# Adaptive modulation units spread into the attention output projection, weight splits by transfer alone, and token blocks formed by ScalarE in a two-layer diffusion trunk on one core

## The chip, the core and the metric

One core of a Trainium2 chip runs the whole program. The metric is the device time of one execution in microseconds, as a median over runs. TensorE (PE) multiplies matrices; VectorE (DVE), ScalarE (ACT) and GpSimd (POOL) do elementwise work. SyncE (SP) and POOL here also issue transfers, each from a queue that it works off in order.

## The reference, cut to what matters

The trunk has two layers over 512 latent and 128 context tokens, 640 columns in all, with a width of 1024. Every sub-layer is modulated by nine vectors that come from the condition, and ends in a LayerNorm:

```python
mod = (silu(cond) @ ada_w[i] + ada_b[i]).reshape(-1, 9, 1024)
x = layer_norm(a*x + 0.5*mod[:, 2]*swiglu(modulate(x, mod[:, 0], mod[:, 1])), ...)
x = layer_norm(a*x + mod[:, 5]*mixer(modulate(x, mod[:, 3], mod[:, 4])), ...)   # attention, or Hyena
x = layer_norm(a*x + 0.5*mod[:, 8]*swiglu(modulate(x, mod[:, 6], mod[:, 7])), ...)
```

Each feed-forward multiplies by w1 (1024 to 2 x 2816), forms silu(g)*u, and multiplies by w2 (2816 to 1024). All arithmetic is in float32.

## The kernel before, in words

**Precision and weights.** Each float32 product is three matmuls: high part by high part, high by low, and low by high. A weight unit is one tile of the stream `units`, for w1 128 x 2048 (1 MB), and it needs a high tile `wh` and a low tile `wl` out of a ring of 8 buffers. The usual way (L120, L137, L138): POOL issues a load that casts to the high part (`wh`), ACT writes its negative into `wl`, and POOL issues a second transfer of the same weights that adds the original onto it. For the odd blocks 3 to 17 of the second feed-forward of layer 0 (`PLAIN`, 8 units) it is done otherwise: SP loads the unit plainly into a third buffer `wr`, ACT casts it to `wh` (L96), and DVE subtracts to get `wl` (L97), in two halves.

**Order.** The schedule is written out by hand; every engine runs its instructions in the order in which the program emits them. `w_get` keeps up to three units split ahead. Small chains (a LayerNorm) are woven into the matmul loops with `at(delay, key, fn)`, by a clock of modelled matmul time, and `flush(key)` emits what is still pending.

**Stages.** Filter spectra; feed-forward (0,0); attention with its output projection (`proj`); feed-forward (0,1); the first feed-forward of layer 1 (`ffn_s(0)`); Hyena with its projection; the last feed-forward (`ffn_s(1)`). A w1 unit is used twice, for token halves 0 and 1, and each use is a step of 48 matmuls. The first three units run half 0 first and half 1 after that (steps 0 to 5), so that the LayerNorm of half 1 has time.

**Modulation units.** One unit is a 128 x 1024 block of `ada_w` (512 KB, tile `ar`, two buffers) that POOL loads (L253) and DVE multiplies and sums against the condition with two instructions (L267), one for latents and one for context. `bg_step` does one unit and asks POOL for the next but one; that request can only go out when DVE has finished with the buffer, and whatever POOL has queued behind it waits too. Feed-forward (0,0) does 56 units (one after each step from block 3 on, and one after each pair of w2 groups); feed-forward (0,1) does 72, with two after each pair of w2 groups in its first two parts. The pool `fq` of that second batch (with `cond`, 1 MB, loaded anew and put through Silu by ACT, L261) is opened when `proj` is done.

**Layer 1's feed-forwards** run the first three w1 blocks in the ordinary way, then w2 for them (`second`, 16 groups of 9 matmuls), and all further blocks by a Strassen-like scheme with 7 products in place of 8. It needs four combinations of token blocks, which `s_tokens(k)` forms for k = 0 to 3: POOL adds high and low parts back to float32 (L596, 4 adds for each k), DVE makes 4 sums and differences (L598 to L601), and 4 splits follow (ACT L96, DVE L97). The calls come after steps 3, 4 and 5, and the last one inside `second`. The LayerNorm's own scale and bias (`s4`, L403, DVE) are put on x after 50 us of modelled time or at the flush ahead of `second`, whose residual updates (L515) need them.

Of the kernel before, what the change touches and what calls it, by code (L numbers as in the profile page):

```python
# [9 lines left out]
F32 = mybir.dt.float32  # L10
F32R = mybir.dt.float32r
# [4 lines left out]
P = 128  # L16
# [4 lines left out]
KD = 8  # L21
# [1 line left out]
NF = 22  # L23
PARTS = [(0, 6), (6, 12), (12, 18), (18, 22)]

PLAIN = range(3, 18, 2)
PARTS7 = [(0, 3), (3, 6), (6, 9), (9, 12), (12, 15), (15, 18), (18, 22)]
ALPHA = 4.0 ** 0.25
EPS = 1e-5
# [16 lines left out]
class Kernel:  # L46
# [63 lines left out]
    def w_dma(self, upto):  # L110
        nc = self.nc
        while self.wd < min(upto, self.wlim):
            i = self.wd
            src, shape, plain = self.units[i]
            if plain:
                r = self.wp.tile(shape, F32, tag="w", name="wr")
                nc.sync.dma_start(out=r, in_=src)
            else:
                r = self.wp.tile(shape, F32R, tag="w", name="wh")
                nc.gpsimd.dma_start(out=r, in_=src)  # L120
            self.raw[i] = r
            self.wd += 1

    def w_split(self):
        i = self.ws
        if i >= self.wlim:
            return
        self.w_dma(i + 1)
        shape, plain = self.units[i][1:]
        hi = self.raw.pop(i)  # L130
        lo = self.wp.tile(shape, F32R, tag="w", name="wl")
        if plain:
            raw, hi = hi, self.wp.tile(shape, F32R, tag="w", name="wh")
            for k in (slice(0, KD // 2), slice(KD // 2, KD)):
                self.split(hi[:, k], lo[:, k], raw[:, k])
        else:
            self.nc.scalar.activation(out=lo, in_=hi.bitcast(F32), func=AF.Copy, scale=-1.0)  # L137
            self.nc.gpsimd.dma_start(out=lo, in_=self.units[i][0], accum_op=ALU.add)  # L138
        self.wt[i] = (hi, lo)
        self.wlive.add(i)  # L140
        self.ws += 1
        self.w_dma(i + 3)

    def w_first(self):

        i = self.wd
        src, shape = self.units[i][:2]
        self.raw[i] = self.wp.tile(shape, F32, tag="w", name="wr")
        self.nc.sync.dma_start(out=self.raw[i], in_=src)
        self.wd += 1  # L150
# [199 lines left out]
    def ln_sched(self, l, i, half, sum_t, GB):  # L350
        nc = self.nc
        a, z = HALF[half]
        C = (z - a) // 4
        key = f"ln{half}"
        when = LNT[min(2 * l + i, 2)][half]
        st = {}

        def s1():
            mu = self.ps(name="mu")
            nc.tensor.matmul(mu[:, 0:320], self.ones_mean, sum_t)  # L360
            sq = {}
# [12 lines left out]

            self.interleave([[lambda k=k: centre(k), lambda k=k: square(k), lambda: None, lambda k=k: add(k)] for k in range(KD)])
            (nc.vector if half else nc.gpsimd).tensor_tensor(out=sq[4], in0=sq[0], in1=sq[4], op=ALU.add)
            st["q"] = sq[4]

        def s2():
            vp = self.ps(name="vp")  # L380
            for c in range(4):
                nc.tensor.matmul(vp[:C, c:c + 1], st["q"][:, c * C:(c + 1) * C], self.ones_mean[:, 0:1])
            st["dg"] = self.rstd(vp, C)

        def s3():
            r = self.ps(name="rs")
            for c in range(4):
                nc.tensor.matmul(r[:, c * C:(c + 1) * C], self.ones[:C, :], st["dg"][:, c, :])
            if half == 0:
                self.h = []  # L390
            G, B = GB

            def scale(k):
                xk = self.x[:, k, a:z]
                nc.vector.tensor_tensor(out=xk, in0=xk, in1=r[:, 0:320], op=ALU.mult)

            self.interleave([[lambda k=k: scale(k)] + self.h_stages(half, k, self.x[:, k, :], G, B) for k in range(KD)],
                            key, when[3])

        def s4():  # L400
            for k in range(KD):
                xk = self.x[:, k, a:z]
                nc.vector.tensor_scalar(out=xk, in0=xk, scalar1=self.lnga[:, l, i, k:k + 1],  # L403
                                        scalar2=self.lnba[:, l, i, k:k + 1], op0=ALU.mult, op1=ALU.add)

        for t, f in zip(when, (s1, s2, s3)):
            self.at(t, key, f)
        self.at(50, key + "x", s4)

    def ln_out(self, l, i, half, sum_t):  # L410

# [175 lines left out]
    def s_tokens(self, k):  # L587

        nc = self.nc
        B = {}  # L590
        for r in range(2):
            hh, hl = self.h[k + 4 * r]
            for c in range(2):
                cs = slice(320 * c, 320 * c + 320)
                B[r, c] = self.t((P, 320), name="sb")
                nc.gpsimd.tensor_tensor(out=B[r, c], in0=hh[:, cs].bitcast(F32), in1=hl[:, cs].bitcast(F32), op=ALU.add)  # L596
        t1, t3, t2, t4 = B[0, 0], B[0, 1], B[1, 1], B[1, 0]
        nc.vector.tensor_tensor(out=t1, in0=t3, in1=t1, op=ALU.subtract)  # L598
        nc.vector.tensor_tensor(out=t3, in0=t2, in1=t3, op=ALU.subtract)
        nc.vector.tensor_tensor(out=t2, in0=t2, in1=t1, op=ALU.subtract)  # L600
# [119 lines left out]
    def ffn_s(self, f, u0):  # L720
# [27 lines left out]
        acts = {}  # L748
        self.wlim = u + 5
        steps = self.group_steps(range(u, u + 3), lambda w, q, half, u=u: self.ffn1(acts, q - u, sact)(w, q, half))  # L750
        for n, s in enumerate(steps):
            self.run_steps([s])
            if n == 2:
                self.s_load(3, 0)
                self.s_load(3, 1)
            if n > 2:
                self.s_tokens(n - 3)
        self.flush("ln0x")
        self.flush("ln1x")
        gt = self.gate(l, 2 + 3 * (2 if f else 0), 0.5)  # L760
        w = self.s_weights(3, 4)
        second(u + 3, acts, gt, {1: lambda: self.s_tokens(3), 6: w[0], 8: w[1], 10: w[2], 12: w[3]})
        u += 5
        for pi, (c0, c1) in enumerate(PARTS7[1:]):
            fin = pi == 5
            acts = {}
            for i in range(3):
# [7 lines left out]
                    w = self.s_weights(c + 1, after[c + 1])  # L775
                    hooks = {0: w[0], 1: w[1], 3: w[2], 5: w[3]}
                if i == 1:
                    hooks[2] = lambda m=u + 1: cast(m)
                    hooks[3] = lambda m=u + 2, w=w: (w[2](), cast(m))
                if i == 2:  # L780
                    hooks[0] = self.w_split
# [37 lines left out]
    def ffn(self, l, f, u0):  # L819
# [8 lines left out]
        for pi, part in enumerate(PARTS):  # L828
# [2 lines left out]
            c = part[0]  # L831
            while c < part[1] - fin:
                n = 3 if c == 0 else 1
                self.run_steps(self.group_steps(range(u, u + n), lambda w, q, half, d=c - u: ffn1(q + d)(w, q, half)), c > 0)
                u += n
                c += n
            if pi == 0:
# [4 lines left out]
            if not fin:  # L842
                for jj in range(4):
                    w = self.w_get(u)
                    for j2 in range(2):
                        for half in range(2):
                            ps = self.ps(name="f")
                            self.mm_cols(ps, w, j2 * P, acts, ks, half)
                            self.resid(ps, jj * 2 + j2, half, gt)
                        self.bg_step()  # L850
                        if pi < 2 and f:
                            self.bg_step()
                    self.w_done(u)
                    u += 1
            else:
# [6 lines left out]
                def fn(w, q, half, u=u, c=c):  # L862
# [11 lines left out]
                        self.ln_out(l, i_ln, half, sums[half])  # L874
                    elif j == 7:
                        self.ln_sched(l, i_ln, half, sums[half], GB)
                self.run_steps(self.group_steps(range(u, u + 3), fn))
                u += 3
        return u

# [27 lines left out]
    def attn(self, u0):  # L908
# [215 lines left out]
        for x in late:  # L1124
            av(*x)
        self.wmax = 3
        return self.proj(u + 6, o, gt, 0, 1, ())


    def sin_layer(self, ps, bias, out, m):  # L1130
# [668 lines left out]
    def proj(self, u, z, gt, l, i_ln, late):  # L1799
# [17 lines left out]
                self.ln_sched(l, i_ln, half, sums[half], GB)  # L1817
        self.flush("ln0x")
        self.flush("ln1x")
        self.run_steps(self.group_steps([u], fn))  # L1820
        GB = self.sh(l, i_ln)
        self.run_steps(self.group_steps([u + 1, u + 2, u + 3], fn))
        return u + 4

    def run(self):
        nc, tc, I, O = self.nc, self.tc, self.I, self.O
        with ExitStack() as es:
# [13 lines left out]
            for l in range(2):  # L1841
# [5 lines left out]
                    units += [(I["hyin"][j], [P, KD, 256]) for j in range(12)]  # L1847
                    units += [(I["hyout"][j], [P, KD, 256]) for j in range(4)]
                self.add_ffn_units(units, l, 1)
            self.w_init([(x + (False,))[:3] for x in units])  # L1850
            self.consts()
            with tc.tile_pool(name="fp", bufs=1) as self.fp:
                self.x2d = dp.tile([KD, P, T], F32, name="x2d")
# [2 lines left out]

                self.spectra()
            with tc.tile_pool(name="fa", bufs=1) as fa:
                self.ada_pool(fa, 7 * KD)
                u = self.ffn(0, 0, 0)  # L1860
                self.need_mods(0, [3, 4, 5, 6, 7, 8])
            with tc.tile_pool(name="ap", bufs=1) as self.ap:
                u = self.attn(u)
            with tc.tile_pool(name="fq", bufs=1) as fq:
                self.ada_pool(fq, 16 * KD)
                u = self.ffn(0, 1, u)
                self.need_mods(1, range(9))
            with tc.tile_pool(name="s0", bufs=1) as self.sp:
# [8 lines left out]
    def add_ffn_units(self, units, l, f):  # L1877
# [8 lines left out]
            return  # L1886
        for pi, (p0, p1) in enumerate(PARTS):
            for c in range(p0, p1):
                units.append((I["w1"][l, f, c], [P, KD, 256], f == 1 and c in PLAIN))
# [160 lines left out]
```

## Time and profile before

| what | value |
|---|---|
| median of 3 runs (lowest, highest) | 2765.34 us (2765.14, 2765.74) |
| the profiled execution's own time | 2762.68 us |
| its span, first to last instruction | 2760.7 us |
| PE busy | 2611.2 us, 95% |
| DVE / ACT / POOL busy | 1722.9 / 1031.3 / 752.7 us |
| mean granted PE clock | 0.978 of full |
| HBM read / written | 418.39 / 16.01 MB |

The profile is of one execution. "Idle before <-X" is time in which an engine stood still until X let it go on. Where PE is never idle and its clock is full, a stage is as short as its matmuls allow; time is lost where PE waits, and in the clock after that.

### The profile page before, as it was taken

To read this page: it belongs to the slowest core of one execution; us is meant where nothing else is said; L and a number is where in the kernel's file an instruction comes from. 1 tells how busy PE (TensorE), PEld (TensorE's weight loads), DVE (VectorE), ACT (ScalarE), POOL (GpSimd) and SP (SyncE) were. 2 spreads that over 40 slices of the span, in tenths; PEclk is the share of its full clock that TensorE was granted. 3 is DMA by queue.
4 is the path that set the end of the run, shared out by engine and by line. 5 is a ranking of instruction groups with operands and counts; after the bars stand their busy time and mean duration, and the time that the engine had idled before them with its cause. 6 is when DMAs were issued, how large, how long until landed. Compare 5 with 4: busy or idle time off the path is not lost. (4 is left out here: it accounts for less than half of the span.)

```text
span 2760.7 us, 43283 instructions
## 1 busy us (share of the span) xinstructions
PE 2611.2 (95%) x16970; PEld 2472.4 (90%) x16970; DVE 1722.9 (62%) x3616; ACT 1031.3 (37%) x1780; POOL 752.7 (27%) x1002
## 2 busy tenths in 40 slices
PE   8889999999899998989999999999999899999997
PEld 3679999998746898989999999999999899999997
DVE  5855565628864456667637766665437947766664
ACT  3762222125675331212124434443422324434442
POOL 3521211224122411111224111114116844111113
PEclk9999999999999999999999999999999999999998
DMA  7767988854302556776854656666654354656663
GB/s 247 206 195 212 270 218 246 231 143 118 83 16 77 153 139 207 207 216 207 244 144 94 145 134 153 159 147 167 153 152 143 118 160 98 138 141 153 151 151 85
DMA packets 101507, 443.24 MB, mean 161 GB/s; under 512 B 12095, under 2 KB 17807, under 8 KB 77496
## 3 DMA queue, kind: packets, MB, share of 16 engines
q0 software_dynamic: 69312, 342.33, 49.3%
q1 hardware_dynamic: 31624, 98.11, 10.0%
q8 instruction: 134, 2.20, 0.3%
q14 instruction: 69, 0.57, 0.1%
q10 hardware_dynamic: 368, 0.04, 0.0%
HBM read 418.39 MB, written 16.01 MB: 157 GB/s over the span
## 5 line engine op out<-in xcount | busy, mean ns | idle before, releaser
L515 DVE SCALAR_TENSOR_TENSOR x<-f,gate,x 128x192 f32<-128x192 f32 (+2 forms) x576 | 227.5, 434 | 184.7 <-PE f L534 184.1
L534 PE MATMUL f<-sa,wh 128*128 128x320 f32 (+2 forms) x1344 | 304.0, 313 | 15.8 <-DVE sa L97 10.6
L137 ACT ACTIVATE wl<-wh 128x2048 fp32r<-128x2048 f32 (+1 forms) x123 | 214.0, 1740 | 271.2 <-PE f L534 161.3
L573 PE MATMUL g<-hh,wl 128*128 128x320 f32 (+1 forms) x832 | 260.6, 313 | 29.5 <-DMA wl<-w 29.5
L573 PE MATMUL g<-hh,wh 128*128 128x320 f32 (+1 forms) x832 | 260.6, 313 | 0.0
L573 PE MATMUL u<-hh,wh 128*128 128x320 f32 (+1 forms) x832 | 259.3, 312 | 0.0
L676 PE MATMUL sm<-st,sw 128*128 128x320 f32 x1728 | 259.3, 309 | 0.0
L573 PE MATMUL u<-hl,wh 128*128 128x320 f32 (+1 forms) x832 | 259.2, 312 | 0.0
L573 PE MATMUL g<-hl,wh 128*128 128x320 f32 (+1 forms) x832 | 259.0, 311 | 0.0
L573 PE MATMUL u<-hh,wl 128*128 128x320 f32 (+1 forms) x832 | 259.0, 311 | 0.0
L676 PEld LDWEIGHTS sm<-st,sw 128*128 128x128 f32 x1728 | 254.9, 188 | 0.0
L534 PEld LDWEIGHTS f<-sa,wh 128*128 128x128 f32 x1344 | 230.1, 192 | 17.6 <-DVE sa L97 11.1
L534 PE MATMUL f<-ah,wl 128*128 128x320 f32 (+2 forms) x736 | 229.7, 312 | 6.2 <-DMA wl<-w2a 6.2
L534 PE MATMUL f<-al,wh 128*128 128x320 f32 (+2 forms) x736 | 229.8, 312 | 2.0 <-DVE al L97 1.6
L534 PE MATMUL f<-ah,wh 128*128 128x320 f32 (+2 forms) x736 | 230.3, 313 | 0.0
L253 POOL DMA_DIRECT2D ar<-ada_w x128 | 68.2, 533 | 569.9 <-DVE mods L267 559.8
L267 DVE CUSTOM_DVE_ANT_0 prod<-ar,cond,ab 128x1024 f32<-128x1024 f32 x128 | 163.9, 1280 | 95.4 <-DMA ar<-ada_w 92.5
L534 PE MATMUL f<-sa,wl 128*128 128x320 f32 (+2 forms) x672 | 210.4, 313 | 3.5 <-DMA wl<-w2c 3.1
L676 PE MATMUL sm<-hh,sw 128*128 128x320 f32 x864 | 197.9, 309 | 0.0
L582 DVE TENSOR_TENSOR ac<-sg,u 128x320 f32<-128x320 f32 (+1 forms) x104 | 50.5, 486 | 230.0 <-ACT sg L580 230.0
L573 PEld LDWEIGHTS g<-hh,wl 128*128 128x128 f32 x832 | 158.1, 190 | 31.7 <-DMA wl<-w 31.7
L580 ACT ACTIVATE sg<-g 128x320 f32<-128x320 f32 (+1 forms) x104 | 45.1, 434 | 341.2 <-PE g L573 341.1
(362 smaller groups left out, 6852.8 us busy)
## 6 DMA issues: line engine op xcount, KB each, us to landing
ar<-ada_w POOLq DMA_DIRECT2D x128, 512.0 KB, 5.6
wh<-w POOLq DMA_DIRECT2D x42, 1024.0 KB, 12.0
wl<-w POOLq DMA_DIRECT2D x42, 1024.0 KB, 10.1
sr<-w1s SPq DMA_DIRECT2D x72, 512.0 KB
wh<-w2a POOLq DMA_DIRECT2D x24, 768.0 KB, 10.8
wl<-w2a POOLq DMA_DIRECT2D x24, 768.0 KB, 9.4
wh<-w2c POOLq DMA_DIRECT2D x24, 768.0 KB, 8.8
wl<-w2c POOLq DMA_DIRECT2D x24, 768.0 KB, 6.8
```

Source lines behind the costliest of these rows:

```text
L137: self.nc.scalar.activation(out=lo, in_=hi.bitcast(F32), func=AF.Copy, scale=-1.0)
L253: self.nc.gpsimd.dma_start(out=self.ada_raw[n], in_=self.I["ada_w"][l, m, j])
L267: nc.vector.tensor_tensor_reduce(out=out, in0=w, in1=self.cond[:, tk], scale=1.0, scalar=self.ab[:, l, m, j:j + 1], op0=ALU.mult, op1=ALU. ...
L515: nc.vector.scalar_tensor_tensor(out=self.x[:, j, s0:s1], in0=ps[:, s0 - a:s1 - a], scalar=gate[:, tk, j:j + 1], in1=self.x[:, j, s0:s1], ...
L534: nc.tensor.matmul(ps[:, 0:z - a], s[:, kw, c0:c0 + P], m[:, a:z], start=(first and i == 0 and q == 0), stop=(last and i == n - 1 and q == 2))
L573: nc.tensor.matmul(o[:, 0:z - a], s[:, k, c0:c0 + P], m[:, a:z], start=(k == 0 and q == 0), stop=(k == 7 and q == 2))
L580: nc.scalar.activation(out=sg, in_=g[:, 0:z - a], func=AF.Silu)
L582: nc.vector.tensor_tensor(out=ac, in0=sg, in1=uu[:, 0:z - a], op=ALU.mult)
L676: nc.tensor.matmul(ps[:, 0:320], s[:, k], x, start=(k == 0 and q == 0), stop=(k == 3 and q == 2))
```

## The change

It does five things. (1) `PLAIN` goes: all weight units take the load, ACT negation and adding transfer. (2) The modulation units are spread anew: feed-forward (0,0) does 60, beginning after step 3; the pool `fq` is opened after attention and before `proj`, `proj` does one unit after each of its 8 steps, and feed-forward (0,1) begins after its step 3 and does one, never two, at a time. (3) `s_tokens` computes the blocks on ACT as G*x + B from the normalised x, in place of POOL's adds; for token half 0 this is one instruction of 320 columns, for half 1 two of 192 and 128. (4) `s_tokens(k)` is emitted ahead of steps 3, 4 and 5 and after step 5, with nothing of it inside `second`; `s4` of the two LayerNorms ahead of layer 1's feed-forwards waits for the flush, and for half 1 it is done by ACT. (5) A load of w2 is emitted one product earlier (hook 1 in place of 2).

```diff
-            src, shape, plain = self.units[i]
-            if plain:
-                r = self.wp.tile(shape, F32, tag="w", name="wr")
-                nc.sync.dma_start(out=r, in_=src)
-            else:
-                r = self.wp.tile(shape, F32R, tag="w", name="wh")
-                nc.gpsimd.dma_start(out=r, in_=src)
+            src, shape = self.units[i]
+            r = self.wp.tile(shape, F32R, tag="w", name="wh")
+            nc.gpsimd.dma_start(out=r, in_=src)
...
-        self.at(50, key + "x", s4)
+        self.at(1e6 if blocks else 50, key + "x", s4)
...
+                if blocks and half:
+                    nc.scalar.activation(out=xk, in_=xk, func=AF.Identity, scale=w, bias=b)
+                else:
+                    nc.vector.tensor_scalar(out=xk, in0=xk, scalar1=w, scalar2=b, op0=ALU.mult, op1=ALU.add)
...
     def s_tokens(self, k):
...
-                nc.gpsimd.tensor_tensor(out=B[r, c], in0=hh[:, cs].bitcast(F32), in1=hl[:, cs].bitcast(F32), op=ALU.add)
+                for s0, s1, tk in SEG[c]:
+                    nc.scalar.activation(out=o[:, s0 - a:s1 - a], in_=self.x[:, kk, s0:s1], func=AF.Identity,
+                                         scale=G[:, tk, kk:kk + 1], bias=B[:, tk, kk:kk + 1])
...
     def ffn_s(self, f, u0):
...
+            if n == 3:
+                self.flush("ln1")
+            if n >= 3:
+                self.s_tokens(n - 3)
+            self.run_steps([x])
...
-            if n > 2:
-                self.s_tokens(n - 3)
+        self.s_tokens(3)
...
-        second(u + 3, acts, gt, {1: lambda: self.s_tokens(3), 6: w[0], 8: w[1], 10: w[2], 12: w[3]})
+        second(u + 3, acts, gt, {6: w[0], 8: w[1], 10: w[2], 12: w[3]})
...
-                    hooks[2] = lambda m=u + 1: cast(m)
+                    hooks[1] = lambda m=u + 1, w=w: (w[1](), cast(m))
...
     def ffn(self, l, f, u0):
...
+                self.run_steps(steps[:n if c == 0 else 0])
+                self.run_steps(steps[n if c == 0 else 0:], True)
...
                         self.bg_step()
-                        if pi < 2 and f:
-                            self.bg_step()
...
     def proj(self, u, z, gt, l, i_ln, late):
...
-        self.run_steps(self.group_steps([u], fn))
+        self.run_steps(self.group_steps([u], fn), True)
         GB = self.sh(l, i_ln)
-        self.run_steps(self.group_steps([u + 1, u + 2, u + 3], fn))
+        self.run_steps(self.group_steps([u + 1, u + 2, u + 3], fn), True)
...
-                self.ada_pool(fa, 7 * KD)
+                self.ada_pool(fa, 7 * KD + 4)
...
             with tc.tile_pool(name="ap", bufs=1) as self.ap:
-                u = self.attn(u)
+                u, o, gt = self.attn(u)
             with tc.tile_pool(name="fq", bufs=1) as fq:
                 self.ada_pool(fq, 16 * KD)
+                u = self.proj(u, o, gt, 0, 1, ())
                 u = self.ffn(0, 1, u)
```

## Rows read from the trace of the kernel before

**Rows 1.** Windows: length, busy us (count) PE PEld DVE ACT POOL, clock, DMA, GB/s.

```profile
303.00:429.00 126.00, 126.00 (x861) 126.00 (x860) 73.63 (x133) 27.28 (x33) 27.31 (x44) 1.00 0.88 248
...
1029.00:1173.00 144.00, 129.19 (x832) 128.40 (x831) 95.31 (x164) 27.17 (x37) 24.50 (x41) 0.93 0.67 202
```

**Rows 2.** Timeline of ACT: Silu ending a w1 step (start, duration).

```profile
252.45 0.44 ACT L580 ACTIVATE sg<-g 128x320 f32<-128x320 f32 x1 [5.57 <-PE g L573]
...
598.14 0.44 ACT L580 ACTIVATE sg<-g 128x320 f32<-128x320 f32 x1 [3.77 <-PE g L573]
...
1028.66 0.44 ACT L580 ACTIVATE sg<-g 128x320 f32<-128x320 f32 x1 [5.58 <-PE g L573]
...
1416.68 0.44 ACT L580 ACTIVATE sg<-g 128x320 f32<-128x320 f32 x1 [3.77 <-PE g L573]
```

**Rows 3.** Waits of PE, 1029 to 1318: total us, times, longest.

```profile
PE g L573 <- DMA wl<-w: 23.8, 4, 6.6
PE f L534 <- DMA wl<-w2a: 6.2, 2, 3.7
```

**Rows 4.** POOL's timeline in (0,1); PE's waits 176 to 303.

```profile
1219.31 0.53 POOL L253 DMA_DIRECT2D ar<-ada_w  x1 [2.00 <-DVE mods L267]
1219.83 0.92 POOL L138 DMA_DIRECT2D wl<-w  x1
...
PE g L573 <- DMA wl<-w: 0.4, 1, 0.4
```

**Rows 5.** Start of (0,0): POOL, ACT; landing of L138; its median.

```profile
199.87 0.91 POOL L138 DMA_DIRECT2D wl<-w  x1 [11.75 <-ACT wl L137]
...
223.46 0.54 POOL L253 DMA_DIRECT2D ar<-ada_w  x1 [8.21 <-DVE mods L267]
...
210.21 0.44 ACT L580 ACTIVATE sg<-g 128x320 f32<-128x320 f32 x1 [3.78 <-PE g L573]
...
218.62 1.90 ACT L261 ACTIVATE cond<-cond 128x2048 f32<-128x2048 f32 x1
...
DMA to landing us min/median/max: 8.4/8.4/8.4
...
wl<-w POOLq DMA_DIRECT2D x42, 1024.0 KB, 10.1
```

**Rows 6.** Projection: timelines of ACT, PE; transfers issued 872 to 946.

```profile
894.15 1.92 ACT L137 ACTIVATE wl<-wh 128x2048 fp32r<-128x2048 f32 x1 [11.96 <-DMA wh<-wo]
...
904.43 0.41 PE L534 MATMUL f<-oh,wl 128*128 128x320 f32 x1 [2.34 <-DMA wl<-wo]
...
cond<-cB POOLq DMA_DIRECT2D x1, 1024.0 KB, 5.1
```

**Rows 7.** PE's waits 940 to 990; window 955 to 960.

```profile
PE g L573 <- DMA wl<-w: 3.0, 1, 3.0
...
955.00:960.00 5.00, 4.90 (x19) 4.90 (x20) 0.15 (x1) 0.00 (x0) 0.00 (x0) 0.50 0.26 102
```

**Rows 8.** Layer 1's start: PE's waits 1480 to 1535; POOL, DVE.

```profile
PE f L534 <- DVE sa L97: 5.3, 1, 5.3
PE f L534 <- DVE x L515: 2.9, 2, 1.8
...
1505.97 6.05 POOL L596 TENSOR_TENSOR sb<-hh,hl 128x320 f32<-128x320 f32 x7
...
1506.43 5.95 DVE L97 TENSOR_TENSOR sa<-ac,sa 128x320 fp32r<-128x320 f32 x1 [0.54 <-ACT sa L96]
```

**Rows 9.** Timeline of ACT in the same stage.

```profile
1451.75 0.64 ACT L322 ACTIVATE h<-x,B,G 128x320 f32<-128x320 f32 x1
1452.29 0.46 ACT L325 ACTIVATE hh<-h 128x320 fp32r<-128x320 f32 x1
...
1490.31 1.55 ACT L96 ACTIVATE st<-sb 128x320 fp32r<-128x320 f32 x4 [2.08 <-DVE sb L600]
...
1535.00 0.44 ACT L692 ACTIVATE s<-sm 128x320 f32<-128x320 f32 x1 [1.25 <-PE sm L676]
```

More of the change, by code (lines that the diff above doesn't have):

```diff
@@ L24 @@
 PARTS = [(0, 6), (6, 12), (12, 18), (18, 22)]
-PLAIN = range(3, 18, 2)
 PARTS7 = [(0, 3), (3, 6), (6, 9), (9, 12), (12, 15), (15, 18), (18, 22)]
@@ L128, in w_split @@
         self.w_dma(i + 1)
-        shape, plain = self.units[i][1:]
+        shape = self.units[i][1]
         hi = self.raw.pop(i)
         lo = self.wp.tile(shape, F32R, tag="w", name="wl")
[L132 to L138, printed above, removed]
+        self.nc.scalar.activation(out=lo, in_=hi.bitcast(F32), func=AF.Copy, scale=-1.0)
+        self.nc.gpsimd.dma_start(out=lo, in_=self.units[i][0], accum_op=ALU.add)
         self.wt[i] = (hi, lo)
@@ L146, in w_first @@
         i = self.wd
-        src, shape = self.units[i][:2]
+        src, shape = self.units[i]
         self.raw[i] = self.wp.tile(shape, F32, tag="w", name="wr")
@@ L390, in s3 @@
                 self.h = []
-            G, B = GB
+            G, B = self.gb = GB
             def scale(k):
@@ L398, in s3 @@
                             key, when[3])
+        blocks = (l, i) in ((0, 2), (1, 1))
         def s4():
@@ L402, in s4 @@
                 xk = self.x[:, k, a:z]
-                nc.vector.tensor_scalar(out=xk, in0=xk, scalar1=self.lnga[:, l, i, k:k + 1],
-                                        scalar2=self.lnba[:, l, i, k:k + 1], op0=ALU.mult, op1=ALU.add)
+                w, b = self.lnga[:, l, i, k:k + 1], self.lnba[:, l, i, k:k + 1]
+                if blocks and half:
+                    nc.scalar.activation(out=xk, in_=xk, func=AF.Identity, scale=w, bias=b)
+                else:
+                    nc.vector.tensor_scalar(out=xk, in0=xk, scalar1=w, scalar2=b, op0=ALU.mult, op1=ALU.add)
         for t, f in zip(when, (s1, s2, s3)):
             self.at(t, key, f)
-        self.at(50, key + "x", s4)
+        self.at(1e6 if blocks else 50, key + "x", s4)
     def ln_out(self, l, i, half, sum_t):
@@ L589, in s_tokens @@
         nc = self.nc
-        B = {}
+        G, B = self.gb
+        b = {}
         for r in range(2):
-            hh, hl = self.h[k + 4 * r]
             for c in range(2):
-                cs = slice(320 * c, 320 * c + 320)
-                B[r, c] = self.t((P, 320), name="sb")
-                nc.gpsimd.tensor_tensor(out=B[r, c], in0=hh[:, cs].bitcast(F32), in1=hl[:, cs].bitcast(F32), op=ALU.add)
-        t1, t3, t2, t4 = B[0, 0], B[0, 1], B[1, 1], B[1, 0]
+                o = b[r, c] = self.t((P, 320), name="sb")
+                kk, a = k + 4 * r, HALF[c][0]
+                for s0, s1, tk in SEG[c]:
+                    nc.scalar.activation(out=o[:, s0 - a:s1 - a], in_=self.x[:, kk, s0:s1], func=AF.Identity,
+                                         scale=G[:, tk, kk:kk + 1], bias=B[:, tk, kk:kk + 1])
+        t1, t3, t2, t4 = b[0, 0], b[0, 1], b[1, 1], b[1, 0]
         nc.vector.tensor_tensor(out=t1, in0=t3, in1=t1, op=ALU.subtract)
@@ L750, in ffn_s @@
         steps = self.group_steps(range(u, u + 3), lambda w, q, half, u=u: self.ffn1(acts, q - u, sact)(w, q, half))
-        for n, s in enumerate(steps):
-            self.run_steps([s])
+        for n, x in enumerate(steps):
+            if n == 3:
[3 more added lines that the diff above has]
+            self.run_steps([x])
             if n == 2:
@@ L833, in ffn @@
                 n = 3 if c == 0 else 1
-                self.run_steps(self.group_steps(range(u, u + n), lambda w, q, half, d=c - u: ffn1(q + d)(w, q, half)), c > 0)
+                steps = self.group_steps(range(u, u + n), lambda w, q, half, d=c - u: ffn1(q + d)(w, q, half))
+                self.run_steps(steps[:n if c == 0 else 0])
+                self.run_steps(steps[n if c == 0 else 0:], True)
                 u += n
@@ L876, in fn @@
                         self.ln_sched(l, i_ln, half, sums[half], GB)
-                self.run_steps(self.group_steps(range(u, u + 3), fn))
+                self.run_steps(self.group_steps(range(u, u + 3), fn), True)
                 u += 3
@@ L1126, in attn @@
         self.wmax = 3
-        return self.proj(u + 6, o, gt, 0, 1, ())
+        return u + 6, o, gt
     def sin_layer(self, ps, bias, out, m):
@@ L1849, in run @@
                 self.add_ffn_units(units, l, 1)
-            self.w_init([(x + (False,))[:3] for x in units])
+            self.w_init(units)
             self.consts()
@@ L1858, in run @@
             with tc.tile_pool(name="fa", bufs=1) as fa:
-                self.ada_pool(fa, 7 * KD)
+                self.ada_pool(fa, 7 * KD + 4)
                 u = self.ffn(0, 0, 0)
-                self.need_mods(0, [3, 4, 5, 6, 7, 8])
+                while self.ada_n < self.ada_end:
+                    self.bg_step()
             with tc.tile_pool(name="ap", bufs=1) as self.ap:
-                u = self.attn(u)
+                u, o, gt = self.attn(u)
             with tc.tile_pool(name="fq", bufs=1) as fq:
                 self.ada_pool(fq, 16 * KD)
+                u = self.proj(u, o, gt, 0, 1, ())
                 u = self.ffn(0, 1, u)
@@ L1888, in add_ffn_units @@
             for c in range(p0, p1):
-                units.append((I["w1"][l, f, c], [P, KD, 256], f == 1 and c in PLAIN))
+                units.append((I["w1"][l, f, c], [P, KD, 256]))
             if pi < 3:
```

## The prediction, made before the changed kernel ran

> **What bounds the kernel now.** First the windows. PE works through feed-forward (0,0) at 861 matmuls in 126.0 us, 0.146 us each, with the clock at 1.00; the like stretch of feed-forward (0,1) has 832 in 144 us, with PE busy for 129.2 us and the clock at 0.93 [rows 1]. The reader is to see that the matmuls alone set the time in the one stage, and something else in the other. How much: from the end of the last step of part 0 to the first step of part 3 the stages do the same matmuls. In (0,0) that takes 598.14 - 252.45 = 345.7 us, in (0,1) 1416.68 - 1028.66 = 388.0 [rows 2]. So 42.3 us are lost there, the largest loss in any stage that the change touches.
>
> Then the waits. PE waited 23.8 us in 4 pieces for the low part of a w1 unit and 6.2 for that of w2 [rows 3]. POOL's timeline shows the link: the request for a late unit goes out 0.5 us behind a modulation request that POOL could not issue until DVE had finished with the buffer; at the like place of (0,0) PE waited 0.4 us [rows 4]. With 30.0 us of waits out of 42.3, the other 12 are the half clock after them (1.2 of 2.4 GHz; mean 0.93) [rows 1, 3].
>
> Last, the start of layer 1's feed-forwards, where PE waits 5.3 us for the low part of an activation and 2.9 for a residual [rows 8]. That low part took DVE 5.95 us, where others of its form take 0.49; it ended within 0.1 us of a run of seven POOL adds [rows 8]. It is POOL's adds that hold DVE up.
>
> **Feed-forward (0,1): -42.3 us.** After the change its code from step 3 on is that of (0,0): the same transfers, one modulation unit at a time, no third buffer, no DVE subtraction. So I take the whole 42.3 [rows 2]. Below, nothing more can be won, as (0,0) runs at the rate of its matmuls; above, I keep 15 us back in case the first unit of a part stays late. In (0,0) the negation is hidden on ACT (27 of 126 us busy) and the transfers in a DMA share of 0.88 [rows 1]; without that cover each late unit would cost 6 us and its half clock.
>
> **Starts of the two feed-forwards: +2.5 us.** In (0,0) units now begin after step 3, not step 6. ACT puts Silu of the condition (1.9 us) ahead of the negation for block 3, and POOL's next modulation request goes out 223.46 - 218.62 = 4.8 us after that Silu begins [rows 5]. It began right behind the last split of a step; 1.4 us into the next one, at 197.5, it puts POOL at 202.3, and block 3's adding transfer, at 199.87 before, at 202.9. With the 8.4 us that it takes to land and 1.3 for the 512 KB now ahead of it (the first two blocks of that stage, issued back to back, land 1.3 apart), it lands at 212.5; PE wants it 0.3 us behind the step that ends at 210.2 [rows 5]. That is 2.0 us late. With the median landing of 10.1 in place of 8.4 [rows 5] it would be 3.7; with none of the 512 KB in the way, 0.8. In (0,1) the Silu is over by then: 0.5, from 0 to 3. The later blocks have 14 us for each unit, so they catch up.
>
> **Attention's projection: +3 us.** `cond` and two blocks (2 MB) now go out as soon as attention is over, ahead of the weights for the last projection unit. Before, ACT began its negation at 894.15, the moment its high part landed, and PE waited 2.34 us for its low part at 904.43 [rows 6]. So this chain had no slack: 2 MB ahead of the high part add some 5 us (`cond` alone lands after 5.1), and two refills ahead of the low part up to 2.6 more, at the 1.3 used above. I take 4.5 us, and 1 for the half clock. In the LayerNorm woven into the last three steps, each unit puts 2 x 1.28 us on DVE between links of the chain; two of them fall into it, with up to 3.5 us of slack ahead of the first step: +1.5. Against it, `cond` and its blocks no longer stand ahead of the third w1 unit, where PE waited 3.0 us and then ran at a clock of 0.50 for 5 us [rows 7]: -4. Bounds: -5 (the relief alone) and +13 (all of the 2 MB and both refills on the path, half clock, no slack).
>
> The Trainium skill ("SBUF — State Buffer", section "SBUF: two separate sides") says that GpSimd and a DVE operation with two SBUF inputs take a shared port pair in turn, whichever starts first holding it for its whole instruction. The trace agrees with blocking: 5.95 us where 0.49 is usual [rows 8]. By that rule the L267 instructions in `proj` would also stand behind POOL's sums of squares there; it would add some 3 us to this term, and my sum goes by the rows without it.
>
> **Layer 1's feed-forwards: -5 us for both.** The POOL adds go, and with them the blocked DVE instruction. But all of it now lies on ACT's queue, in front of the Silu of the step. One `s_tokens` there: an instruction of 320 columns holds ACT 0.54 us to the next one's start [rows 9], one of 192 some 0.44 in the same timeline, and one of 128 an estimated 0.38 by the slope between them; twice the three is 2.7 us. Two DVE subtractions after the last one (1.1) and four copies (1.55 [rows 9]) make 5.4. A step's Silu and split hold ACT 1.5, a w2 negation 1.5 on the last two steps. That is 6.9 to 8.4 us per step against PE's 48 x 0.146 = 7.0, so ACT falls behind. From 1485.4, where the LayerNorm and step 2 free ACT: blocks to 1490.8, step 3 to 1492.3, blocks to 1497.7, negation and step 4 to 1500.6, blocks to 1506.0, negation 1507.4, step 5's low part at 1509.4. PE ran dry at 1507.2, 5.3 us ahead of the end of DVE's blocked instruction [rows 8]: a wait of 2.2 in place of 5.3. Next late are the residuals: the last blocks end on ACT at 1514.3, DVE's scale and bias of half 0 (eight, 2.9 us) at 1517.6, the first residual at 1518.4. PE has filled all eight accumulators at 1513.8, so it waits 4.6 us, and runs some 2 us late from the half clock. `second` then ends at about 1530.8; before, it ended at 1535.00 less 12 matmuls, 1533.2 [rows 9]. I take 2.5 us for each of the two stages. Bounds for each: -11.6 (no wait and full clock left: 1533.2 against 1500.5 plus 144 matmuls) and +3.5 (each of four block sets 1.5 us dearer).
>
> **The rest: 0.** Hook 1 in place of 2: POOL has nothing between the two, so its queue keeps its order. The added `True` in Hyena's projection and in the last groups does nothing, since all units are done by then. Four more units in (0,0) fill slots that were free (DVE busy 74 of 126 us [rows 1]).
>
> **The sum.** 2762.7 - 42.3 + 2.5 + 3 - 5 = 2720.9 us for the profiled execution; the median lies 2.7 above that execution, so 2723.6, and I say 2723.
>
> **Rivals.** *ACT keeps up* in layer 1: if the Identity instructions overlap better than the rows show, both waits go, and 2 x 9 us more are won: 2706. For it: ACT does nothing else in these 30 us; against it: the queue worked out above has no slack. *The projection pays*: the chain without slack [rows 6] takes the whole 2 MB and the LayerNorm starts late: +13 in place of +3, with 5 us of waits behind it, 2738. *Part of the loss stays*: PE waited in (0,1) because POOL's weight transfers stand behind its modulation requests, and that order remains; if the first unit of each part stays 5 us late with its half clock, 20 us come back: 2743. In (0,0), however, with this very order, PE waited 0.4 us [rows 4].
>
> *Slower*: eight loads move from SP to POOL's queue, and each brings a second pass of 1 MB. If passes no longer overlapped in (0,1), each w1 unit would cost two landings, some 2 x 10.1 = 20.2 us [rows 5], against the 96 x 0.146 = 14.1 of its matmuls: 19 units by 6.1 us are +116 less the 42.3 already lost there, so 2839. It decides once the transfers fill the time; the share in (0,0) is 0.88 [rows 1], so 14% more would be needed, and it comes out slower than before once a unit is 2.2 us late, 42.3 / 19. The same bytes run through (0,0) without it. *No effect*: the 42.3 us come from something that both versions share; against it stands that only the doubled units and the plain loads differ between the two stages.
>
> **How the numbers follow.** My forecast (2714 to 2731) 0.56; ACT keeps up 0.16; the projection pays 0.13; part of the loss stays 0.10; slower 0.03; no effect 0.02. The median can tell about 0.2%, 5.5 us, from no change, so faster is 0.95, same 0.02, slower 0.03. The range takes in the first and second rival and most of the third with the bounds of the terms: 2704 to 2741.
>
> **What would show it.** Right: steps of (0,1) 7.04 us apart without a PE wait for `wl<-w` or `wl<-w2a`, clock 1.00 from 1029 on; a new wait of about 2 us near 210; one of 5 to 8 for `wl<-wo`; at the start of layer 1's feed-forwards no DVE instruction of several us, a short wait for `sa` and a longer one for the residual. Wrong: PE waits for `wl<-w` at the first unit of each part (the 42.3 was not the doubled units); no wait at all at the residual (ACT is faster than its rows); several waits in the projection beyond 8 us.

## The result, and the profile after

The change makes the kernel faster: 2725.56 us (2721.47 to 2726.66, 4 runs) against 2765.24 (2761.09 to 2765.74, 4 runs), a ratio of 0.9857, 95% interval 0.984 to 0.9874. That is 39.7 us less; 42 were forecast. The profiled execution took 2726.66 us; its span is 2724.9, 35.8 shorter than before.

Both kernels run the same matmuls in the same order, so the same Silu can be found in either, and a stage is the time from one Silu to the next. Windows of the kernel after, feed-forward (0,0) and the same 144 us past the end of part 0 of (0,1), columns as in [rows 1]:

```profile
303.00:429.00 126.00, 126.00 (x861) 126.00 (x860) 70.98 (x128) 27.70 (x34) 24.53 (x40) 1.00 0.83 232
1044.00:1188.00 144.00, 144.00 (x983) 144.00 (x983) 83.03 (x152) 31.13 (x38) 29.76 (x47) 1.00 0.82 230
```

In those 144 us PE now does 983 matmuls instead of 832, is never idle, and the clock is 1.00. The Silu that answer to [rows 2]:

```profile
255.81 0.44 ACT L575 ACTIVATE sg<-g 128x320 f32<-128x320 f32 x1 [5.58 <-PE g L568]
...
600.77 0.44 ACT L575 ACTIVATE sg<-g 128x320 f32<-128x320 f32 x1 [3.78 <-PE g L568]
...
1043.66 0.44 ACT L575 ACTIVATE sg<-g 128x320 f32<-128x320 f32 x1 [5.58 <-PE g L568]
...
1388.62 0.44 ACT L575 ACTIVATE sg<-g 128x320 f32<-128x320 f32 x1 [3.78 <-PE g L568]
```

(0,0) takes 600.77 - 255.81 = 344.96 us there, (0,1) 1388.62 - 1043.66 = 344.96: to the hundredth the same, where before they were 345.7 and 388.0. The waits moved elsewhere. PE's waits after, at the start of (0,0), from 880 to 985, and in layer 1's first feed-forward (1440 to 1530):

```profile
PE g L568 <- DMA wl<-w: 2.4, 1, 2.4
...
PE f L529 <- DMA wl<-wo: 5.6, 1, 5.6
PE g L568 <- DMA wl<-w: 3.0, 1, 3.0
PE rs L378 <- DVE dg L500: 2.5, 1, 2.5
PE mu L350 <- POOL sum L517: 2.1, 2, 1.2
...
PE f L529 <- DMA wl<-w2c: 5.7, 1, 5.7
```

The stages that the change touches, each from two rows of a timeline of one profiled execution. (a) Silu of step 5 to that of the next block in (0,0); (b) first matmul with wo to Silu of step 2 of (0,1); (c) from there to the end of part 0; (d) on to the last step but one of part 3, as in [rows 2]; (e), (f) first Silu of layer 1's first and last feed-forward to the first product of the Strassen-like scheme that ScalarE copies.

| kernel | (a) | (b) | (c) | (d) | (e) | (f) |
|---|---|---|---|---|---|---|
| before | 7.04 | 97.26 | 60.42 | 388.02 | 67.80 | 69.39 |
| after | 11.20 | 107.81 | 62.17 | 344.96 | 64.23 | 64.95 |
| difference | +4.16 | +10.55 | +1.75 | -43.06 | -3.57 | -4.44 |
| forecast | +2.0 | +3 | +0.5 | -42.3 | -2.5 | -2.5 |
| two units at a time | 11.55 | 107.70 | 63.54 | 391.15 | 64.50 | 64.51 |
| ... and blocks asked for by SP | 7.56 | 100.46 | 60.43 | 367.22 | 64.36 | 64.18 |
| plain loads back | 10.71 | 105.80 | 60.42 | 344.96 | 64.60 | 65.17 |
| pool after projection | 11.43 | 99.26 | 66.63 | 344.96 | 64.84 | 64.19 |
| loads only | 10.99 | 96.97 | 61.99 | 344.96 | 64.18 | 64.48 |
| late pool, early Silu | 8.88 | 93.36 | 61.67 | 344.96 | 64.17 | 64.58 |
| after, blocks asked for by SP | 7.68 | 102.68 | 60.42 | 344.96 | 64.15 | 64.38 |
| late pool, early Silu, SP | 7.04 | 91.19 | 60.42 | 344.96 | 65.18 | 64.67 |
| ... and negation first | 7.04 | 94.98 | 60.42 | 344.96 | 66.52 | 66.12 |
| POOL forms the blocks | 11.42 | 107.48 | 62.26 | 344.96 | 67.36 | 68.90 |
| reordered start | 11.63 | 107.71 | 60.41 | 344.96 | 61.82 | 61.86 |
| ... with ScalarE's scale | 11.61 | 107.78 | 61.57 | 344.96 | 65.06 | 65.29 |

Kernels that share the code of (c) differ by up to 3 us there (60.41 to 63.54), so a microsecond or two in one cell prove nothing; several in a cell, together with the wait that makes them, do. The stages of the difference row sum to -34.6 of the span's -35.8.

### The profile page after: what moved, and what is told of

Same layout as the page of the kernel before. It is cut to its first block, busy times and chain, and to the rows that moved or that the text cites. A ratio compares the mean times of both kernels' runs of the same rounds, so it can differ in the third digit from the quotient of the medians.

```text
span 2724.9 us, 43301 instructions
## 1 busy us (share of the span) xinstructions
PE 2604.1 (96%) x16970; PEld 2468.2 (91%) x16970; DVE 1684.7 (62%) x3584; ACT 1061.0 (39%) x1836; POOL 742.6 (27%) x986
## 5 line engine op out<-in xcount | busy, mean ns | idle before, releaser
L127 ACT ACTIVATE wl<-wh 128x2048 fp32r<-128x2048 f32 (+1 forms) x131 | 229.2, 1750 | 259.1 <-PE f L529 220.0
L257 DVE CUSTOM_DVE_ANT_0 ar<-ar,cond,ab 128x1024 f32<-128x1024 f32 x128 | 167.8, 1311 | 4.6
```

Source lines behind the costliest of these rows:

```text
L257: nc.vector.tensor_tensor_reduce(out=out, in0=w, in1=self.cond[:, tk], scale=1.0, scalar=self.ab[:, l, m, j:j + 1], op0=ALU.mult, op1=ALU. ...
```

## The experiments

All edits are to the kernel after. Ratios are to the kernel before, run on the same chip; the chips differ by some 7 us (2759.31 to 2766.11 us for before), so ratios are compared rather than times.

**1. What made (0,1) slow: doubled units or plain loads?** Doubled:

```diff
                         self.bg_step()
+                        if pi < 2 and f:
+                            self.bg_step()
```

> The kernel after, with two modulation units again after each pair of w2 groups in the first two parts of feed-forward (0,1); no plain loads. Theory A (two units in a row hold POOL's queue, so the weight transfers behind them come late): 25 to 43 us of the 42 come back, with PE waits for wl<-w and wl<-w2a at the first unit of parts 1 and 2. Rival B (the plain loads were the cause: third buffer, DVE subtraction, second queue): within 5 us of the kernel after, no such wait.

Plain loads back (units 3, 5, ... 17 of (0,1)):

```diff
+            if plain:
+                r = self.wp.tile(shape, F32, tag="w", name="wr")
+                nc.sync.dma_start(out=r, in_=src)
...
+        if plain:
+            raw, hi = hi, self.wp.tile(shape, F32R, tag="w", name="wh")
+            for k in (slice(0, KD // 2), slice(KD // 2, KD)):
+                self.split(hi[:, k], lo[:, k], raw[:, k])
```

> The kernel after, with the 8 plain loads of feed-forward (0,1) again, and one modulation unit at a time. Theory A (the doubled units): within 5 us of the kernel after. Rival B (the plain loads): 25 to 43 us come back. Were it both together, neither this run nor the one with doubled units would give back more than some 10 us.

Doubled: 2770.75 us, 1.0018 (1.0005 to 1.003), so the whole gain is gone; (d) is 46.2 us longer. Plain: 2721.08, 0.9842 (0.9827 to 0.9857); (d) is the same to the hundredth. The doubled units did it, alone. PE's waits from 985 to 1440 with doubled units:

```profile
PE g L568 <- DMA wl<-w: 30.4, 7, 7.7
PE f L529 <- DMA wl<-w2a: 2.1, 1, 2.1
```

POOL's timeline at one of them:

```profile
1088.09 0.53 POOL L243 DMA_DIRECT2D ar<-ada_w  x1 [9.46 <-DVE mods L257]
1090.63 0.53 POOL L243 DMA_DIRECT2D ar<-ada_w  x1 [2.00 <-DVE mods L257]
1091.15 0.92 POOL L128 DMA_DIRECT2D wl<-w  x1
```

The weight's adding transfer goes out 0.5 us behind the second of two requests that stood 9.46 and 2.00 us for DVE, as in [rows 4].

**2. Is it the order of POOL's queue, or the bytes and DVE's work?** The doubled kernel with one word changed:

```diff
-            self.nc.gpsimd.dma_start(out=self.ada_raw[n], in_=self.I["ada_w"][l, m, j])
+            self.nc.sync.dma_start(out=self.ada_raw[n], in_=self.I["ada_w"][l, m, j])
```

> The run with doubled modulation units in feed-forward (0,1), but with the blocks of ada_w requested from SP's queue in place of POOL's; bytes, DVE work and order are otherwise the same. Theory A (a modulation request that waits for its buffer holds POOL's queue, and the weight transfers behind it): of the 45 us that the doubling cost at least 35 go, so 2720 to 2735 us. Rival (the doubled bytes or the doubled DVE work are too much for the w2 groups): they stay, 2755 us or more.

2734.19 us, 0.991 (0.9893 to 0.9926). In (d) 23.9 of the 46.2 us are back. In ratio it is 0.0108 of the 0.0161 that the doubling cost, some 30 of 45 us, but part of this lies in (a), (b) and (c), which the doubling does not touch. The kernel after with the same word changed (0.9839, experiment 4) is the fair measure: against it the doubling costs 0.0071, some 20 us. So about half of the loss went, less than the 35 us expected. In (d) no weight is late any more, and another wait is there. PE's waits from 985 to 1440:

```profile
PE g L568 <- DVE x L510: 15.1, 4, 6.5
PE f L529 <- DVE x L510: 1.6, 2, 1.2
...
```

DVE's timeline there, and the window in which it stands (columns as in [rows 1]):

```profile
1076.39 1.28 DVE L257 CUSTOM_DVE_ANT_0 prod<-ar,cond,ab 128x1024 f32<-128x1024 f32 x1 [4.46 <-DMA ar<-ada_w]
...
1078.93 1.13 DVE L510 SCALAR_TENSOR_TENSOR x<-f,gate,x 128x320 f32<-128x320 f32 x3
...
1072.00:1076.40 4.40, 2.42 (x17) 2.16 (x15) 0.01 (x1) 1.91 (x1) 0.00 (x0) 1.00 1.03 408
```

DVE stands 4.46 us for a block of `ada_w` that has not landed, and the residuals behind it hold the accumulators that PE wants. It is the same pattern on another engine: a queue worked off in order, with something at its head that waits. So theory A holds for about half. The rest fits the rival's bytes as well as the two buffers: while DVE stands there the DMA engines are busy without a break (share 1.03, at 408 GB/s), but a third buffer would have let the request go out earlier. No run tells these two apart.

The one word changes more than the order. SP's transfers go through a queue that the traces call hardware_dynamic, POOL's through software_dynamic, and from 1051 to 1395 the adding transfers of w1 land in a median of 8.0 us where they took 10.0. How much of the half is the order, and how much this, is not shown.

The Trainium skill ("DMA: Bandwidth & Descriptors", section "Issuing engines are not separate DMA queues") says that transfers started from several engines share the same 16 DMA engines, and that starting them from more than one only saves the usually small time of initiating them. Here the measurement decides otherwise: 23.9 us of (d) came from the choice of the issuing engine.

**3. The projection.** No unit in it, with the loads where they were; and the pool opened behind it:

```diff
-        self.run_steps(self.group_steps([u], fn), True)
+        self.run_steps(self.group_steps([u], fn))
...
-                self.ada_pool(fa, 7 * KD + 4)
+                self.ada_pool(fa, 7 * KD + 7)
```

> The kernel after, with the pool fq still opened ahead of the output projection (cond and two blocks, 2 MB, loaded there), but no modulation unit done in it: (0,0) does 63, (0,1) 65. Theory A (two separate costs): the PE wait for wl<-wo stays near 5 us, as cond and its blocks still stand ahead of wo, and the waits for mu and rs in the LayerNorm shrink to some 1.5 us in all, so the projection takes 4 to 6 us less than in the kernel after. Rival (the units cost nothing there and the loads everything): the projection as long as in the kernel after, within 1.5 us.

```diff
-                self.ada_pool(fq, 16 * KD)
                 u = self.proj(u, o, gt, 0, 1, ())
+                self.ada_pool(fq, 16 * KD)
```

> The kernel after, with the pool fq opened after the output projection as in the kernel before, and no modulation unit in the projection: feed-forward (0,0) does 63 units, (0,1) 65 from its step 3 on, the last two in its final group. Theory A (the projection's +10.7 us come from the 2 MB ahead of wo and from the units in its LayerNorm): 9 to 12 us less than the kernel after, in the profile between the first matmul of the projection and the first of (0,1). Rival (the loss lies in something else there, or moves into (0,1) where cond then stands ahead of its weights): less than 4 us gained.

Loads only: 2714.54 us, 0.9825 (0.9801 to 0.9849). Pool after: 2721.44, 0.9843 (0.9821 to 0.9864). The window of (b), after, then with the loads only (columns as in [rows 1]):

```profile
873.68:981.49 107.81, 93.96 (x590) 91.23 (x590) 65.49 (x141) 36.48 (x62) 55.80 (x73) 0.92 0.67 186
```

```profile
871.70:968.67 96.97, 89.61 (x590) 87.46 (x590) 40.22 (x109) 34.59 (x61) 44.15 (x66) 0.96 0.60 163
```

PE's waits with the loads only, 870 to 985:

```profile
PE f L529 <- DMA wl<-wo: 5.2, 1, 5.2
...
PE rs L378 <- DVE dg L500: 1.2, 1, 1.2
PE mu L350 <- POOL sum L517: 0.3, 1, 0.3
```

In (b) the eight units cost all of it: 10.8 us, 6.5 as idle time (107.81 - 93.96 = 13.85 against 7.36) and 4.4 as slower matmuls (PE busy 93.96 against 89.61, clock 0.92 against 0.96). The early loads alone cost nothing on balance: (b) is 96.97 against 97.26 before. The wait for wo grows from 2.34 [rows 6] to 5.2, and the wait of 3.0 for the third w1 unit [rows 7] goes. The expected 4 to 6 us was too little, as I had left that unit's 3 us out. With the pool behind the projection, (b) falls to 99.26, but (c) rises to 66.63, and 4.5 of the 8.5 us are given back, as the rival of that run had it. The first unit's DVE work then comes only behind the Silu of `cond` in (0,1), and POOL's timeline shows what that holds up:

```profile
986.68 0.60 POOL L243 DMA_DIRECT2D ar<-ada_w  x1 [11.64 <-DVE mods L257]
987.28 0.99 POOL L128 DMA_DIRECT2D wl<-w  x1
```

**4. Nothing but order.** No unit in the projection, the pool's loads behind those of wo, and the Silu ahead of step 3:

```diff
+        steps = self.group_steps([u + 1, u + 2, u + 3], fn)
+        self.run_steps(steps[:2])
+        if i_ln == 1 and l == 0:
+            self.ada_pool(self.fq, 16 * KD)
+        self.run_steps(steps[2:])
...
                 self.run_steps(steps[:n if c == 0 else 0])
+                self.cond_silu()
```

> The kernel after, with no modulation unit in the projection, the pool fq's loads put behind those of wo (after the second of the last six steps), and Silu of the condition put ahead of step 3 of both layer-0 feed-forwards. (0,0) does 63 units, (0,1) 65. Theory A (what was lost is a matter of order alone): the wait for wl<-wo back to 2 to 3 us, none above 1.5 in the LayerNorm, none for the third w1 unit, and none of over 0.7 us at block 3 of either feed-forward: 12 to 16 us less than the kernel after, 2710 to 2714. Rival (the start of (0,1) takes the waits over, as it did with the pool opened behind the projection): 3 to 7 us less.

2708.62 us, 0.9795 (0.9778 to 0.9812): 17 us under the kernel after, more than expected. (b) is 93.36, 3.9 below the kernel before. The wait for wo is 2.9 us, and of the waits that were to go only those at block 3 of (0,0) and (0,1) stayed, at 1.6 and 1.0 us. Two runs put the requests on SP's queue (the one-word diff above), in the kernel after and in this one:

> The kernel after, with the blocks of ada_w requested from SP's queue. By theory A the wait for the third w1 unit ahead of (0,1), 3.0 us and its half clock, goes, as its adding transfer no longer stands behind a held request; the waits at block 3 of both feed-forwards shrink to under 1.5 us; the units' DVE work in the LayerNorm still costs its 4 us: 4 to 9 us less than the kernel after. Rival (the order of the queue does not matter there): within 3 us.

> The version with the pool opened late in the projection and the early Silu (2708.62 us), with the blocks of ada_w requested from SP's queue. Theory A: the adding transfer of block 3 goes out behind ScalarE's negation and no longer behind a modulation request, so its waits of 1.6 and 1.0 us go: 1 to 4 us less. Rival (those two waits come from the 512 KB that land with it, whichever queue asks for them): within 1 us.

The kernel after so edited took 2714.97 us, 0.9839 (0.9821 to 0.9858), an interval that overlaps that of the kernel after; in the profiled execution (b) is 5.1 shorter, with no wait for the third w1 unit, and (a) 3.5. The late pool so edited took 2705.46, 0.9812 (0.9797 to 0.9827): PE has no wait at all in 176 to 303 nor in 985 to 1380, (a) and (c) are 7.04 and 60.42. By the ratios it can't be told from the version with POOL's requests, as the intervals overlap; by its stages it is the better one.

**5. Layer 1: does POOL hold DVE up?** POOL's adds again, at the new places:

```diff
+                hh, hl = self.h[kk]
+                nc.gpsimd.tensor_tensor(out=o, in0=hh[:, a:a + 320].bitcast(F32), in1=hl[:, a:a + 320].bitcast(F32), op=ALU.add)
```

> The kernel after, with the token blocks formed by POOL again (high part plus low part), at the places of the kernel after. Theory A (it is POOL's adds that hold DVE's two-input instructions up): DVE instructions of 2 to 6 us appear at the start of layer 1's feed-forwards, and both stages together take 4 to 15 us more. Rival (it was the place of the calls that made the long wait, not the engine): no DVE instruction beyond 2 us there, and with ScalarE's queue free w2's low part is no longer late, so 5 to 10 us less.

2731.04 us, 0.9877 (0.986 to 0.9894), an interval that overlaps that of the kernel after; in the profiled execution (e) and (f) take 3.1 and 4.0 us more. That is nearly all that the change won there (3.57 and 4.44). DVE's timeline, then POOL's:

```profile
1472.82 3.51 DVE L96 TENSOR_TENSOR sa<-ac,sa 128x320 fp32r<-128x320 f32 x1 [0.54 <-ACT sa L95]
```

```profile
1472.38 3.59 POOL L592 TENSOR_TENSOR sb<-hh,hl 128x320 f32<-128x320 f32 x4
```

A DVE subtraction of 0.49 us in the kernel after takes 3.51 here and ends 0.36 us behind the end of four POOL adds in a row. Theory A holds; w2's low part is late here too, by 6.3 us.

**6. Layer 1: what is late next?** The negation of w2's first unit ahead of the second set of blocks, the later sets behind the first residuals, and the scale and bias in pieces:

```diff
+            if n == 4:
+                self.w_get(x[0])
+                self.s_tokens(1)
+                self.s4_after(1)
...
+        second(u + 3, acts, gt, {1: lambda: late(2), 2: lambda: late(3), 6: w[0], 8: w[1], 10: w[2], 12: w[3]})
```

> The kernel after, with the start of layer 1's feed-forwards reordered: the negation of w2's first unit goes on ScalarE ahead of the second set of token blocks, the third and fourth sets go behind the first residuals, and the LayerNorm's own scale and bias are done on VectorE for two of the eight tiles at a time, right behind the set that reads them. Theory A (only ScalarE's queue holds w2's low part back, 5.65 us in each stage): the wait goes, 8 to 14 us less in both stages together. Rival (the next late link, step 5's low part or the first residuals, takes the wait over): less than 5 us.

> The reordered start of layer 1's feed-forwards, with the scale and bias of half 1 left on ScalarE, behind the last set of token blocks, in place of VectorE. Theory A (VectorE's queue, with 16 scale instructions more between the residuals, gave back what the earlier negation won): 3 to 6 us less than the kernel after in the two stages. Rival (the stretch behind runs at the pace of its weight transfers and ScalarE): within 2 us of it, with PE waits for sw<-w1s and wl<-w2c between 1515 and 1545.

2726.55 us, 0.9858 (0.9844 to 0.9873), and 2723.41, 0.985 (0.9831 to 0.9869): no gain that can be told. Reordered, (e) and (f) are 2.4 and 3.1 us shorter, and new waits, in part behind the first product, give it back: ScalarE copies the second product of the first of these stages 78.05 us after its first Silu, and 78.13 in the kernel after. PE's waits there, 1440 to 1530:

```profile
PE f L533 <- DMA wl<-w2c: 2.8, 1, 2.8
PE f L533 <- DVE x L514: 2.0, 1, 2.0
PE sm L683 <- DMA sw<-w1s: 1.1, 1, 1.1
...
```

With the scale on ScalarE the residual's wait goes, and that for `sw` becomes 3.4. The first theory fell both times, the rivals held. The last run took the late pool with SP's queue and the one line that puts the negation first:

```diff
             if n >= 3:
+                self.w_get(x[0])
                 self.s_tokens(n - 3)
```

> The late pool with the early Silu and the blocks of ada_w from SP's queue, and one change more: in layer 1's feed-forwards ScalarE's negation of w2's first unit goes ahead of the second set of token blocks, everything else there as in the kernel after. Theory A for layer 0 (waits at block 3 and for the third w1 unit come from POOL's queue): again none of them over 0.5 us. For layer 1: the wait for wl<-w2c falls from 5.6 to some 2 to 3 us, a wait of 1 to 2 us for step 5's low part or the first residual follows, and the two stages together take 2 to 5 us less than in the kernel after; rival (the residuals set the pace): within 1 us. Together a ratio of 0.978 to 0.981 to the kernel before.

2707.89 us, 0.9795 (0.9782 to 0.9808), with no wait in (a) and (c) again. In layer 1, PE's waits from 1400 to 1530:

```profile
PE f L533 <- DVE x L514: 4.6, 1, 4.6
PE f L533 <- DMA wl<-w2c: 1.7, 2, 1.4
PE f L533 <- ACT sa L95: 0.8, 1, 0.8
...
```

The residual takes the wait over, at 4.6 us, and (e) and (f) are 2.3 and 1.2 us longer than in the kernel after, where 2 to 5 less in all were expected and the rival had no change. So taking w2's wait away by this line alone won nothing: the residuals cost as much.

## Why the prediction was right, and where it was not

**Feed-forward (0,1): right, -43.06 for -42.3.** It had read POOL's queue as the link, named two differences between the stages, doubled units and plain loads, and taken both away at once. (What it calls the first step of part 3 is the last but one; at the first one the stages differ by 42.33 us too.) Experiment 1 says which: only the doubled units, which cost 46.2 us when put back alone. About half of that cost hangs on POOL's queue, and when it is gone DVE waits for blocks (experiment 2). "Part of the loss stays" and "slower" did not come about: the first unit of each part is on time, and the share of the transfers is 0.82.

**Starts: right mechanism, +5.9 for +2.5.** The wait of 2.37 us in (0,0) is near the 2.0 worked out; its half clock, some 1.8 more (4.16 - 2.37; the granted clock is 0.79 from 212 to 220), was left out here, though counted for the projection. In (c) a wait of 1.5 us makes the 1.75, which is within what kernels with the same code differ by. Stage (a) is 8.88 with the Silu moved, 7.68 with SP's queue alone and 7.04 with both: the modulation request ahead of the weight is the larger part.

**The projection: mis-sized, +10.55 for +3, within its bounds.** The early loads come out 1.8 us better than judged: 4.5 + 1 - 4 = +1.5 forecast, -0.3 measured (the wait for wo grew by 2.9, the 3.0 went). The term that failed is "two of them fall into it, with up to 3.5 us of slack ahead of the first step: +1.5". The units cost 10.8. First, they lengthen the LayerNorm chain: PE waits 4.6 us for `rs` and `mu` against 1.5 with loads only. Second, the prediction had the third w1 unit freed by the pool's early opening, and forgot that the units' own requests now stand ahead of it. POOL's timeline after:

```profile
957.22 0.57 POOL L243 DMA_DIRECT2D ar<-ada_w  x1 [1.39 <-DVE mods L257]
957.78 0.95 POOL L128 DMA_DIRECT2D wl<-w  x1
```

That is the very order of [rows 4], and the 3.0 us of [rows 7] stayed. With the units asked for by SP (experiment 4) this wait goes and 5.1 of the 10.8 us with it; the waits for `rs` and `mu` stay at 4.7. So about half is the request in POOL's queue, and the rest the units on DVE. The rival that the projection pays 13 us came near in size, and the sign of several waits beyond 8 us came about (13.2 us in all), but the 2 MB that the rival names was not the cause.

**Layer 1: right sign, -8.0 for -5, with the wrong wait.** "PE ran dry at 1507.2" treats step 5's low part as the first thing wanted, but w2's own low part is wanted by the third matmul with w2, some 6 us earlier. PE's timeline before:

```profile
1500.99 0.31 PE L534 MATMUL f<-sa,wl 128*128 128x320 f32 x1
...
1506.86 0.31 PE L534 MATMUL f<-sa,wh 128*128 128x320 f32 x1
```

The prediction has the negation follow the blocks at 1497.7 and ends its account there; the adding transfer behind it is missing. In the kernel after (ScalarE's timeline):

```profile
1464.49 2.84 ACT L592 ACTIVATE sb<-x,B,G 128x320 f32<-128x320 f32 x6
1468.47 1.55 ACT L95 ACTIVATE st<-sb 128x320 fp32r<-128x320 f32 x4 [1.15 <-DVE sb L597]
1469.93 1.47 ACT L127 ACTIVATE wl<-wh 128x1536 fp32r<-128x1536 f32 x1
```

The request goes out at 1471.71 and lands 7.0 us later; PE goes on at 1478.71 after a wait of 5.65, so it had been ready since 1473.06. The residual's wait of 4.6 us that the prediction worked out does not show, because PE comes to it 5.7 us late; once the negation went first it showed, at 4.6 (experiment 6). Its sign of being wrong, no wait at the residual because ACT is faster than its rows, thus came about, but not for that reason: the rows above take 5.53 us from the first block instruction to the end of the copies, 5.4 were forecast. ScalarE's queue sets the pace, as it said; it put the first wait in the wrong place.

**The rest** came to -1.2 of the span; no run undoes the earlier load of w2 by itself. The terms sum to 6 us too much in the profiled execution (-41.8 against -35.8): the projection and the starts cost 7.6 and 3.4 more than forecast, and layer 1, (0,1) and the rest together won 5.0 more. In the medians they are only 2.1 too much, as this profiled execution lies 1.1 above its median and that of before 2.6 below its own. So it is in part luck that the forecast came so near; the term that carries it, the 42.3, is not.

## What to carry to other kernels

A transfer that waits for a buffer belongs on a queue where nothing urgent stands behind it; asking for it from another engine costs one word and was worth up to 24 us in a stage here. Background work that fits by its busy share can still cost time when it stands inside a chain of short dependent steps: eight units of some 2.6 us on DVE made the projection 10.8 us longer, though DVE was busy for only 65 of its 108 us. Where two units in a row are fed by two buffers, another queue moves the wait rather than ending it. Where a wait goes, follow what was wanted ahead of it, each request through to its landing, before naming what is late next.

## What the runs showed of the hardware

The modulation instruction on DVE (two full SBUF inputs, 128 x 1024) takes 1.28 us alone and up to 2.01 in the projection after, and POOL's `sum<-sum,x` there 1.77 where 0.87 is its undisturbed length. DVE's timeline:

```profile
905.78 1.75 DVE L257 CUSTOM_DVE_ANT_0 ar<-ar,cond,ab 128x1024 f32<-128x1024 f32 x1
908.39 2.01 DVE L257 CUSTOM_DVE_ANT_0 prod<-ar,cond,ab 128x1024 f32<-128x1024 f32 x1
```

The Trainium skill ("SBUF — State Buffer", section "SBUF: two separate sides") says that a DVE instruction with two SBUF inputs and a GpSimd one that reads SBUF take a shared port pair in turn, each for its whole instruction. These rows agree: each grew by less than one instruction of the other (0.73 against 0.87, 0.90 against 1.28). In experiment 5 the measurement goes further: a subtraction of 0.49 us took 3.51 beside four POOL adds and ended behind the last, so it stood behind more than one. The prediction had weighed the rule at 3 us for the projection and left it out of the sum; the runs don't price it apart from the units themselves.
